# One slot for the widest weights, fewer copy transfers, and evenly spread preparation steps in a hybrid DeltaNet and attention layer

## The chip, the cores and the metric

The kernel runs on one core of a Trainium2 chip. A core has five engines that work side by side: TensorE (PE in the profile, its weight loads PEld), VectorE (DVE), ScalarE (ACT), GpSimd (POOL) and SyncE (SP), which issues most DMA transfers. The metric is the device time of one execution in microseconds (us); lower is better. The engines are tied to each other by semaphores: an instruction that lacks an input waits, and so does everything behind it in its engine's queue.

## What is computed

The reference is one layer of a transformer over 1024 latent tokens and 256 context tokens of width 1024:

```python
px = modulate(rms_norm(x, norm1_w[i]), sh1, sc1) @ w_in[i]
pc = modulate(rms_norm(ctx, norm1_w[i]), csh1, csc1) @ w_in[i]
dn_c, s_ctx_f, s_ctx_b = gated_deltanet(pc[..., :DN_IN], ...)
dn_x, _, _ = gated_deltanet(px[..., :DN_IN], ..., s_ctx_f, s_ctx_b)
na_x = neighborhood_attention(qx, kx, vx, kc, vc, na_rpb[i], rows)
x = x + g1 * (jnp.concatenate([dn_x, na_x], axis=-1) @ w_out[i])
x = x + g2 * swiglu(modulate(rms_norm(x, norm2_w[i]), sh2, sc2), w_ffn_in[i], w_ffn_out[i])
```

The columns of the input projection go to two groups. Group A (gated DeltaNet) has 4 heads: a short convolution and SiLU on q, k and v, then a scan over chunks of the sequence, forward and backward. Each chunk needs the inverse of a triangular matrix built from k, the decay and beta. Group B has 8 heads of attention over a window of the 64-wide latent grid together with all context keys.

## The kernel before, in words

**Jobs.** The projection is a list of jobs, worked off in a loop over `n` (L1050 and on). A `Block` makes 128 columns for all tokens: its product (`mm`, L405) runs in 8 parts `k`, each of 6 matmuls (queries, two token segments) or 9 (keys and values, three segments). A `Wide` makes 256 or 272 columns, token tile by token tile (`wide`, L595, 24 matmuls a tile; 10 tiles for the attention's values, 8 for the gate z). In order: `k0 k1 k2 k3 z1 | nk0 nk1 nk2 nv0 nk3 | q0..q3 | nq0..nq3 v0 nv1 | v1 v2 v3 z0`. The number of nk0's job is `inv`, of nq0's `later`, of nv1's `values`. After its product a job is evacuated by ACT (L438, L453), gets SiLU or squares, in the next round a `norm`, two rounds later a `finish`, which for values transposes (L527), scales on DVE (L531) and stores to HBM (L535, array `v_d`).

**Norm of attention keys and queries.** `norm` (L490 to L493) takes for each segment a PSUM bank named "m", does one matmul (L492) and takes the logarithm from the bank on ACT (L493). Keys have three segments. There are two "m" banks, two "pr" banks and four "blk" banks in that phase.

**Background steps.** Two generators run beside the jobs, by `bg.step` (L1090, L1096): `block_inverses` (43 steps: decay tables; masks; an elimination on DVE over 30 columns, L885 and L887, two columns a step; a memset, L891; transposes back on PE, L897; a store to `x_d`) and then `preps` (10 preparations of two chunks each, 8 steps each; matmuls L967, L968, L987, L998 in "pr" banks, stores to `at_d` and `y_d`, L1010). The first two preparations may run early; the other eight wait until all q jobs are finished, which is so from nq2 on. They need 64 steps. A block gives 8 steps, a wide tile 2, a tile of nv1 3. What remains is drained ahead of v3 (L1061).

**Order.** Where no order is written out by hand, the framework's planner orders each engine's instructions: those that come first in the code go first, unless its model says that their inputs are not ready, in which case later ones pass. So the queues differ from the order in the code, and a queue waits where the model was wrong.

**Weights.** Every weight block goes from HBM into the one slot `wraw` (L195, L586), is rounded into a high part by ACT (L199, L587) and its remainder taken by POOL (L200, L588). The Wide jobs' high and low parts lie in one slot `zw` in the pool `zp`, but z0's lie in a new pool `sp1`, opened when `zp` and all other pools of the phase have been closed (L1063 to L1066).

**The turn to the next phase.** With nv1 done, 64 transfers of 64 KB copy its rows from `nv_d` to the window layout `vw_d` (L1104 to L1109) on SP's queue. Ahead of v3 the attention generator `fill` starts its loads (L260, L262, L263: qs, kh, kl). With z0 the PSUM pools change (L1070): z0's product and the attention's first scores (L303) share the new banks. Then the scan starts.

Of the kernel before, what the change touches and what calls it, by code (L numbers as in the profile page):

```python
# [9 lines left out]
F32 = mybir.dt.float32  # L10
F32R = mybir.dt.float32r
# [9 lines left out]
KT = 8  # L21
# [67 lines left out]
def hybrid(ctx, tc, a, dbg):  # L89
# [45 lines left out]
        dve.memset(bias[:, i:i + 1], v)  # L135
    b_eps, b_naq = bias[:, 0:1], bias[:, 1:2]
    mr = const("mr", [128, 5, 128], F32R)
    mneg = const("mneg", [128, 2, 128], F32R)

    v_d = dram.tile([T, 512], F32, name="v_d", tag="v_d")  # L140
    k_d = dram.tile([T, 512], F32, name="k_d", tag="k_d")
# [233 lines left out]
    with ExitStack() as bs:  # L375
# [32 lines left out]
        class Block:  # L408
# [64 lines left out]
            def norm(self):  # L473

                kind, acc, t0, i = self.kind, self.acc, self.t0, self.i
                if kind == "v":
                    return
                if kind == "k":
                    sp.dma_start(kT_d[:, :, i], acc.rearrange("p (c t) -> p c t", t=128))
                    return  # L480
                r = self.r
                if kind == "q":
                    sp.dma_start(qT_d[:, :, i], acc[:, t0:].rearrange("p (c t) -> p c t", t=128))
                    p = bank()
                    for c in range(8):
                        pe.matmul(p[:, c:c + 1], r[:, t0 + c * 128:t0 + (c + 1) * 128], M[C_ONE][:, 0:1],
                                  start=True, stop=True)
                    dve.tensor_copy(SQ[:, :, i], p[:, 0:8])
                    return
                for s0, n in self.segs:  # L490
                    p = bank()
                    pe.matmul(p[:, :n], M[C_BD2], r[:, s0:s0 + n], start=True, stop=True)  # L492
                    act.activation(r[:, s0:s0 + n], p[:, :n], AF.Ln, bias=b_eps, scale=1.0 / ND)  # L493
                if kind == "nq":
                    act.activation(r[:, t0:], r[:, t0:], AF.Exp, scale=-0.5, bias=b_naq)
                else:
                    act.activation(r[:, t0:], r[:, t0:], AF.Exp, scale=-0.5)
                isk = kind == "nk"
                u = acc
                dve.scalar_tensor_tensor(u[:, t0:], u[:, t0:], qkw[:, isk:isk + 1], r[:, t0:],  # L500
                                         op0=OP.mult, op1=OP.mult)
                hl16 = cp.tile([128, 2, T], F16, name="hl16", tag="kx", bufs=3)
                h16, l16 = hl16[:, 0], hl16[:, 1]
                if isk:
                    act.copy(h16, u)
                    dve.tensor_tensor(l16, u, h16, OP.subtract)
                else:
                    for hf in range(2):
                        s = slice(t0 + hf * 512, t0 + hf * 512 + 512)
                        uv = u[:, s].rearrange("p (r b c) -> p b r c", r=8, b=4)  # L510
                        hv, lv = (x[:, s].rearrange("p (b r c) -> p b r c", b=4, r=8) for x in (h16, l16))
                        act.copy(hv, uv)
                        dve.tensor_tensor(lv, uv, hv, OP.subtract)
                for i, x in enumerate((h16, l16)):
                    for hb in range(2):
                        hd = 2 * self.i + hb
                        dst = nk_d[i, hd] if isk else nq_d[hd, i]
                        sp.dma_start(dst, x[hb * 64:hb * 64 + 64, t0:])

            def finish(self):  # L520
                kind, acc, i = self.kind, self.acc, self.i
                if kind in "kv":
                    vt = cp.tile([128, NCH, 128], F32, name="vt", tag="kx", bufs=3)
                    for g, m in ((0, 4), (4, 4), (8, 2)):
                        p = bank()
                        for c in range(m):
                            pe.transpose(p[:, c * 128:(c + 1) * 128], acc[:, (g + c) * 128:(g + c + 1) * 128], ident)  # L527
                        if kind == "k":
                            act.copy(vt[:, g:g + m].rearrange("p c d -> p (c d)"), p[:, :m * 128])
                        else:  # L530
                            dve.tensor_tensor(vt[:, g:g + m], p[:, :m * 128].rearrange("p (c d) -> p c d", d=128),  # L531
                                              SV[:, g:g + m, i:i + 1].to_broadcast([128, m, 128]), OP.mult)
                        yield
                    dst = v_d if kind == "v" else k_d
                    sp.dma_start(dst[:, i * 128:(i + 1) * 128].rearrange("(c p) d -> p c d", p=128), vt)  # L535
                if kind == "q":
                    kT = cp.tile([128, T], F32, name="kTh", tag="kx", bufs=3)
                    sp.dma_start(kT.rearrange("p (c t) -> p c t", t=128), kT_d[:, :, i])
# [25 lines left out]
        class Wide:  # L564


            def __init__(self, kind, half, zp):
                self.kind, self.half, self.zp = kind, half, zp
                self.n = 272 if kind == "z" and half else 256
                self.lasting = kind == "z" and not half  # L570

            def room(self):
                w = self.zp().tile([128, 2, KT, 256 if self.lasting else 272], F32R, name="zw", tag="zw")
                self.hi, self.lo = w[:, 0], w[:, 1]

            def prefetch(self):
                h2, n = 2 * self.half, self.n // 2
                src = a["w_nv"] if self.kind == "nv" else a["w_z%d" % self.half]
                if self.kind == "z":
                    h2 = 0  # L580
                if not self.lasting:
                    self.room()
                for i in range(2):
                    raw = wp.tile([128, KT, 136], F32, name="wraw", tag="wraw", bufs=1)
                    r, s = raw[:, :, :n], slice(i * n, i * n + n)
                    sp.dma_start(r, src[h2 + i])  # L586
                    act.copy(self.hi[:, :, s], r)  # L587
                    pool.tensor_tensor(self.lo[:, :, s], r, self.hi[:, :, s].bitcast(F32), OP.subtract)  # L588
# [55 lines left out]
        with ExitStack() as xs:  # L644
# [65 lines left out]
            with tc.manual_schedule(engines={mybir.EngineType.PE, mybir.EngineType.DVE, mybir.EngineType.Activation}):  # L710
# [30 lines left out]
                for k in range(1, KT):  # L741
# [11 lines left out]
                                ada(q, act.copy)  # L753
                    if k == 5:
                        act.copy(mr[:, 4], ident)
                        for d in range(2):
                            act.mul(mneg[:, d], masks[:, d], -1.0e30)
                        act.copy(mr[:, 0:4], masks)

        cp = pools(bs, "cp", "right")  # L760
        late = ExitStack()
        adp = pools(late, "adp", "left")
        zpool = [pools(late, "zp", "left")]
        first_half = ExitStack()
# [4 lines left out]
        def zp():  # L769
            return zpool[0]  # L770

        def decay_tables(gp):
            def small(name):
# [51 lines left out]
        def block_inverses():  # L825
            with ExitStack() as gs:
# [55 lines left out]
                for c in range(30, 0, -1):  # L882
                    w = 31 - c
                    t = tt[:P, :, :c * w].rearrange("p b (r j) -> p b r j", j=w)
                    dve.tensor_tensor(t, N[:P, :, 0:c, c:c + 1].to_broadcast([P, 4, c, w]),  # L885
                                      N[:P, :, c:c + 1, c + 1:32].to_broadcast([P, 4, c, w]), OP.mult)
                    dve.tensor_tensor(N[:P, :, 0:c, c + 1:32], N[:P, :, 0:c, c + 1:32], t, OP.add)  # L887
                    if c % 2:
                        yield
                flat = N.rearrange("p b r c -> p b (r c)")  # L890
                dve.memset(flat[:P, :, 0:1024:33], 1.0)  # L891
                yield
# [134 lines left out]
                        yield  # L1027
                flush(tick[0] + 2)

        jobs = first + [Block("k", 2), Block("k", 3), Wide("z", 1, zp)]  # L1030
        inv = len(jobs)
        jobs += [Block("nk", i) for i in range(3)] + [Wide("nv", 0, zp), Block("nk", 3)]
# [4 lines left out]
        jobs += [Block("nq", i) for i in range(4)] + [Block("v", 0), Wide("nv", 1, zp)]  # L1037
        values = len(jobs) - 1
        jobs += [Block("v", i) for i in (1, 2, 3)] + [Wide("z", 0, zp)]

        def blk(n):
            return jobs[n] if 0 <= n < len(jobs) and isinstance(jobs[n], Block) else None
# [9 lines left out]
        for n in range(2, len(jobs) + 2):  # L1052
# [7 lines left out]
            if n == len(jobs) - 2:  # L1060
                bg.drain()  # L1061
                bg2.drain()
                late.close()  # L1063
                sp1 = pools(middle, "sp1", "left")
                zpool[0] = sp1
                jobs[n + 1].room()  # L1066
                fill = attention(pools(attn, "nw", "left", 2))
                next(fill)
            if final:
# [7 lines left out]
            if isinstance(j, Wide):  # L1077
                for t, _ in enumerate(j.tiles()):
# [4 lines left out]
                    if t == 4 and nrm:  # L1083
# [3 lines left out]
                        fin = nrm.finish()  # L1087
                        done.add(n - 1)
                        nrm = None
                    bg.step(3 if n == values else 2)  # L1090
            elif j:
                for k in range(KT):
                    j.mm([k])
                    if k >= 3:
                        next(fin, 0)
                    bg.step(1)  # L1096
                    if n > inv + 4:
                        bg2.step(1)
                j.evac()
# [3 lines left out]
            if isinstance(j, Wide) and n == values:  # L1103
                vlat = nv_d[CT:].rearrange("(r c) d -> r c d", c=64)  # L1104
                for cb in range(4):
                    for ch in range(4):
                        for r in range(4):
                            sp.dma_start(vw_d[r * 32:r * 32 + 32, :, cb, ch],
                                         vlat[4 * ch + r, BLKS[cb]:BLKS[cb] + 32].rearrange("c (h d) -> c h d", d=128))  # L1109
            if nrm:  # L1110
                nrm.norm()
            if isinstance(j, Block):
# [665 lines left out]
```

## Time and profile before

| | us |
|---|---|
| median of 3 runs | 1546.32 (1540.7 to 1547.51) |
| the profiled execution | 1549.54 |
| its span, first to last instruction | 1547.5 |
| PE busy in the span | 1479.8 (96%) |
| DVE busy | 994.3 (64%) |
| ACT busy | 727.7 (47%) |

The profile's page begins with the busy time of each engine and a picture of the span in 40 slices, in which "PEclk" is the clock granted to TensorE in tenths of full speed. A busy PE at half clock makes half the progress. Further views are the waits (who waited for whom, in sum), the timeline (instructions in order of time; at the end of a row, in brackets, the idle time before it and what ended it; "SPq" and "ACTq" rows are DMA issues), and windows (busy time and granted clock of a stretch).

### The profile page before, as it was taken

To read this page: it belongs to the slowest core of one execution; us is meant where nothing else is said; L and a number is where in the kernel's file an instruction comes from. 1 tells how busy PE (TensorE), PEld (TensorE's weight loads), DVE (VectorE), ACT (ScalarE), POOL (GpSimd) and SP (SyncE) were. 2 spreads that over 40 slices of the span, in tenths; PEclk is the share of its full clock that TensorE was granted. 3 is DMA by queue.
4 is the path that set the end of the run, shared out by engine and by line. 5 is a ranking of instruction groups with operands and counts; after the bars stand their busy time and mean duration, and the time that the engine had idled before them with its cause. 6 is when DMAs were issued, how large, how long until landed. Compare 5 with 4: busy or idle time off the path is not lost. (4 is left out here: it accounts for less than half of the span.)

```text
span 1547.5 us, 23963 instructions
## 1 busy us (share of the span) xinstructions
PE 1479.8 (96%) x8702; PEld 1235.2 (80%) x8702; DVE 994.3 (64%) x1712; ACT 727.7 (47%) x1404; POOL 233.6 (15%) x286
## 2 busy tenths in 40 slices
PE   6999999899989978999999999999999999999998
PEld 3788787678778867888887878888888888888887
DVE  5774497675554543777986469866665556599652
ACT  5442552635764235666773166333333334354440
POOL 1154500733554010111210000000000000000000
PEclk9999999999999979999999999999999999999999
DMA  9274221577556467899637502632323324698742
GB/s 389 64 217 133 67 72 63 163 212 241 182 169 212 130 174 237 283 288 261 220 102 255 208 34 82 211 102 103 103 102 103 109 100 159 231 381 279 244 144 82
DMA packets 204118, 267.35 MB, mean 173 GB/s; under 512 B 16736, under 2 KB 114528, under 8 KB 202976
## 3 DMA queue, kind: packets, MB, share of 16 engines
q1 hardware_dynamic: 198480, 261.07, 51.7%
q10 hardware_dynamic: 5520, 4.76, 0.9%
q8 instruction: 68, 1.11, 0.3%
q14 instruction: 50, 0.41, 0.1%
HBM read 201.02 MB, written 68.94 MB: 174 GB/s over the span
## 5 line engine op out<-in xcount | busy, mean ns | idle before, releaser
L405 PE MATMUL blk<-hh,whi 128*128 128x512 f32 (+1 forms) x410 | 123.4, 395 | 2.3 <-ACT kk L550 1.4
L1415 ACT CAST uhi<-wq 128x512 fp32r<-128x512 f32 x101 | 61.0, 622 | 133.5 <-issue 84.6
L1415 ACT CAST uhi<-ws 128x512 fp32r<-128x512 f32 x91 | 53.9, 621 | 147.3 <-PE ps L1354 92.9
L405 PE MATMUL blk<-hl,whi 128*128 128x512 f32 (+1 forms) x410 | 116.8, 377 | 0.3 <-DVE hl L707 0.3
L595 PE MATMUL blk<-zw,hh 128*128 128x256 f32 (+1 forms) x576 | 115.0, 293 | 1.3 <-ACT kk L550 1.1
L405 PE MATMUL blk<-hh,wlo 128*128 128x512 f32 (+1 forms) x410 | 114.7, 377 | 0.6 <-POOL wlo L200 0.6
L1416 DVE TENSOR_TENSOR ulo<-wq,uhi 128x512 fp32r<-128x512 f32 x101 | 67.4, 687 | 59.1 <-ACT uhi L1415 34.0
L1354 PE MATMUL ps<-hT,uhi 128*128 128x512 f32 x336 | 103.7, 390 | 0.0
L1354 PE MATMUL ps<-hT,ulo 128*128 128x512 f32 x336 | 103.5, 389 | 0.0
L1354 PE MATMUL ps<-lT,uhi 128*128 128x512 f32 x336 | 103.4, 389 | 0.0
L595 PEld LDWEIGHTS blk<-zw,hh 128*128 128x128 f32 x576 | 92.8, 192 | 5.2 <-ACT kk L550 1.4
L1354 PE MATMUL ps<-hB,uhi 128*128 128x512 f32 x288 | 89.2, 391 | 0.6 <-ACT hB L1529 0.6
L1354 PE MATMUL ps<-lB,uhi 128*128 128x512 f32 x288 | 88.7, 389 | 0.4 <-DVE lB L1530 0.4
L1354 PE MATMUL ps<-hB,ulo 128*128 128x512 f32 x288 | 88.7, 389 | 0.0
L405 PEld LDWEIGHTS blk<-hh,wlo 128*128 128x128 f32 x410 | 72.6, 192 | 15.3 <-POOL wlo L200 0.9
L405 PEld LDWEIGHTS blk<-hl,whi 128*128 128x128 f32 x410 | 72.4, 191 | 14.5 <-DVE hl L707 0.8
L405 PEld LDWEIGHTS blk<-hh,whi 128*128 128x128 f32 x410 | 69.4, 194 | 18.2 <-issue 4.5
L595 PE MATMUL blk<-zw,hl 128*128 128x256 f32 (+1 forms) x288 | 83.2, 289 | 0.0
L1354 PEld LDWEIGHTS ps<-lT,uhi 128*128 128x128 f32 x336 | 63.1, 188 | 13.1
L1354 PEld LDWEIGHTS ps<-hT,ulo 128*128 128x128 f32 x336 | 63.1, 188 | 13.1
L1354 PEld LDWEIGHTS ps<-hT,uhi 128*128 128x128 f32 x336 | 62.9, 188 | 13.0
L200 POOL TENSOR_TENSOR wlo<-wraw,whi 128x1024 fp32r<-128x1024 f32 x18 | 44.7, 2485 | 179.2 <-ACT whi L199 160.7
(359 smaller groups left out, 3540.5 us busy)
## 6 DMA issues: line engine op xcount, KB each, us to landing
wq<-w_fo SPq DMA_DIRECT2D x99, 256.0 KB, 4.2
wq<-w_gu SPq DMA_DIRECT2D x88, 256.0 KB, 2.9
wad<-wa SPq DMA_DIRECT2D x64, 256.0 KB, 4.4
bt<-rpb SPq DMA_DIRECT2D x64, 192.0 KB, 3.8
t_d<-g SPq DMA_DIRECT2D x22, 512.0 KB, 3.6
fr<-t_d SPq DMA_DIRECT2D x44, 256.0 KB, 5.0
f_d<-g SPq DMA_DIRECT2D x33, 256.0 KB, 2.1
fr<-f_d SPq DMA_DIRECT2D x33, 256.0 KB, 3.8
```

The costliest lines, as they stand in the source:

```text
L200: lo_engine.tensor_tensor(o, r, h.bitcast(F32), OP.subtract)
L405: pe.matmul(o, ww[:, k], xx[k][:, s], start=k == 0 and j == 0, stop=k == KT - 1 and j == 2)
L595: pe.matmul(p[:, :c1 - c0], x[k][:, s], ww[:, k, c0:c1], start=k == 0 and j == 0, stop=k == KT - 1 and j == 2)
L1354: pe.matmul(o, w[wi][:, k], x[xi][:, k], start=first and k == 0 and j == 0, stop=k == n - 1 and j == 2, skip_group_check=True)
L1415: act.copy(hi, self.raw[key])
L1416: dve.tensor_tensor(lo, self.raw[key], hi.bitcast(F32), OP.subtract)
```

## The change

Seven edits. (1) The third segment of a key block's norm takes a "pr" bank. (2) `sp1` is opened at the start, below the pools that close, and holds one `zw` slot of 272 columns for all four Wide jobs. (3) `mneg`, a constant of the preparations, moves to a pool that closes with the phase and is computed a little later. (4) The stores to `v_d` are issued by ACT, not SP. (5) `block_inverses` yields twice more ahead of its memset. (6) nv1's tiles give 2 steps; blocks from nq0 on give 10, the added ones at `k` of 2 and 6. (7) The 64 copies to `vw_d` become 16 of 256 KB.

```diff
-                for s0, n in self.segs:
-                    p = bank()
+                for j, (s0, n) in enumerate(self.segs):
+                    p = bank("pr" if j == 2 else "m")
...
-                    sp.dma_start(dst[:, i * 128:(i + 1) * 128].rearrange("(c p) d -> p c d", p=128), vt)
+                    (act if kind == "v" else sp).dma_start(dst[:, i * 128:(i + 1) * 128].rearrange("(c p) d -> p c d", p=128), vt)
...
             def room(self):
-                w = self.zp().tile([128, 2, KT, 256 if self.lasting else 272], F32R, name="zw", tag="zw")
+                w = sp1.tile([128, 2, KT, 272], F32R, name="zw", tag="zw")
...
-                        for d in range(2):
-                            act.mul(mneg[:, d], masks[:, d], -1.0e30)
                         act.copy(mr[:, 0:4], masks)
...
+        sp1 = pools(middle, "sp1", "left")
         adp = pools(late, "adp", "left")
-        zpool = [pools(late, "zp", "left")]
+        mneg = adp.tile([128, 2, 128], F32R, name="mneg", tag="mneg")
+        for d in range(2):
+            act.mul(mneg[:, d], mr[:, d].bitcast(F32), -1.0e30)
...
                     if c % 2:
                         yield
+                yield
+                yield
                 flat = N.rearrange("p b r c -> p b (r c)")
                 dve.memset(flat[:P, :, 0:1024:33], 1.0)
...
                 late.close()
-                sp1 = pools(middle, "sp1", "left")
-                zpool[0] = sp1
-                jobs[n + 1].room()
                 fill = attention(pools(attn, "nw", "left", 2))
...
-                    bg.step(3 if n == values else 2)
+                    bg.step(2)
...
-                    bg.step(1)
+                    bg.step(1 + (n >= later and k in (2, 6)))
...
-                        for r in range(4):
-                            sp.dma_start(vw_d[r * 32:r * 32 + 32, :, cb, ch],
-                                         vlat[4 * ch + r, BLKS[cb]:BLKS[cb] + 32].rearrange("c (h d) -> c h d", d=128))
+                        sp.dma_start(vw_d[:, :, cb, ch].rearrange("(r c) h d -> r c h d", c=32),
+                                     vlat[4 * ch:4 * ch + 4, BLKS[cb]:BLKS[cb] + 32].rearrange(
+                                         "r c (h d) -> r c h d", d=128))
```

More of the change, by code (lines that the diff above doesn't have):

```diff
@@ L137, in hybrid @@
     mr = const("mr", [128, 5, 128], F32R)
-    mneg = const("mneg", [128, 2, 128], F32R)
     v_d = dram.tile([T, 512], F32, name="v_d", tag="v_d")
@@ L564, in hybrid, with __init__ @@
         class Wide:
-            def __init__(self, kind, half, zp):
-                self.kind, self.half, self.zp = kind, half, zp
+            def __init__(self, kind, half):
+                self.kind, self.half = kind, half
                 self.n = 272 if kind == "z" and half else 256
-                self.lasting = kind == "z" and not half
             def room(self):
-                w = self.zp().tile([128, 2, KT, 256 if self.lasting else 272], F32R, name="zw", tag="zw")
+                w = sp1.tile([128, 2, KT, 272], F32R, name="zw", tag="zw")
                 self.hi, self.lo = w[:, 0], w[:, 1]
@@ L580, in prefetch @@
                     h2 = 0
-                if not self.lasting:
-                    self.room()
+                self.room()
                 for i in range(2):
@@ L1028, in preps @@
                 flush(tick[0] + 2)
-        jobs = first + [Block("k", 2), Block("k", 3), Wide("z", 1, zp)]
+        jobs = first + [Block("k", 2), Block("k", 3), Wide("z", 1)]
         inv = len(jobs)
-        jobs += [Block("nk", i) for i in range(3)] + [Wide("nv", 0, zp), Block("nk", 3)]
+        jobs += [Block("nk", i) for i in range(3)] + [Wide("nv", 0), Block("nk", 3)]
         turn = len(jobs)
@@ L1036, in hybrid @@
         queries = range(turn, later)
-        jobs += [Block("nq", i) for i in range(4)] + [Block("v", 0), Wide("nv", 1, zp)]
+        jobs += [Block("nq", i) for i in range(4)] + [Block("v", 0), Wide("nv", 1)]
         values = len(jobs) - 1
-        jobs += [Block("v", i) for i in (1, 2, 3)] + [Wide("z", 0, zp)]
+        jobs += [Block("v", i) for i in (1, 2, 3)] + [Wide("z", 0)]
         def blk(n):
```

2 lines of the change are left out of this document (removed).

## The prediction

> **What bounds the kernel now.** I read the page's busy times and PEclk first, then PE's waits in the projection (150 to 600 us, the only part that the edits reach), the SP queue there, and windows with the granted clock.
>
> ```profile
> span 1547.5 us, 23963 instructions
> PE 1479.8 (96%) x8702; PEld 1235.2 (80%) x8702; DVE 994.3 (64%) x1712; ACT 727.7 (47%) x1404; POOL 233.6 (15%) x286
> PEclk9999999999999979999999999999999999999999
> ...
> PE m L492 <- ACT cr L493: 5.3, 4, 1.4
> PE pr L967 <- POOL rg L957: 2.9, 3, 1.2
> PE m L897 <- DVE N L891: 2.9, 1, 2.9
> PE sc L303 <- DMA kh<-nk_d: 4.5, 1, 4.5
> PE sc L303 <- DVE mx L305: 4.1, 1, 4.1
> PE sc L314 <- DVE bt L309: 2.3, 1, 2.3
> ...
> 548.50:595.30 46.80, 35.66 (x264) 32.38 (x264) 20.30 (x31) 16.84 (x29) 5.27 (x4) 0.82 0.60 167
> 552.30:569.40 17.10, 9.81 (x44) 7.64 (x45) 12.05 (x18) 6.74 (x10) 3.16 (x3) 0.50 0.87 245
> 258.80:265.60 6.80, 6.80 (x38) 6.10 (x37) 0.69 (x1) 3.41 (x8) 0.00 (x0) 0.50 0.01 2
> 430.00:496.00 66.00, 60.42 (x540) 53.55 (x539) 35.66 (x45) 35.80 (x75) 33.04 (x45) 1.00 0.62 192
> 195.00:258.00 63.00, 57.48 (x373) 50.60 (x371) 60.06 (x64) 24.19 (x35) 5.46 (x2) 1.00 0.20 59
> ```
>
> PE is busy 96% of the span, so the change can win only idle PE time and half-clock time. In the window rows the columns are length, then busy time of PE, PEld, DVE, ACT and POOL, then the clock. The weakest stretch is 548.5 to 595.3, where z0 and the attention's start share PE: 46.80 us with 35.66 busy, at a mean clock of 0.82. Three waits (4.5, 4.1, 2.3 us; sum 10.9) are nearly all of the 11.1 idle, and the clock stood at 0.50 for 17.10 us from 552.3.
>
> **Where that stall comes from.** The timelines of SP, ACT, POOL and PE:
>
> ```profile
> 495.88 36.09 SPq L1108 DMA_DIRECT2D vw_d<-nv_d  x53
> 533.18 2.42 SPq L1010 DMA_DIRECT2D y_d<-y  x4
> 535.68 0.61 SPq L586 DMA_DIRECT2D wraw<-w_z  x1
> 545.47 0.37 SPq L535 DMA_DIRECT2D v_d<-vt  x1
> 545.93 0.63 SPq L260 DMA_DIRECT2D qs<-nq_d  x1
> 555.34 0.60 SPq L586 DMA_DIRECT2D wraw<-w_z  x1
> ...
> SPq L535 <- DVE vt L531: 9.1, 1, 9.1
> ...
> 517.64 2.38 POOL L200 TENSOR_TENSOR wlo<-wraw,whi 128x1024 fp32r<-128x1024 f32 x1 [17.36 <-PE pr L998]
> 548.13 1.35 ACT L453 COPY cr<-blk 128x256 f32<-128x256 f32 x3 [5.77 <-PE blk L405]
> 549.35 1.07 ACT L587 CAST zw<-wraw 128x1024 fp32r<-128x1024 f32 x1
> 550.50 2.34 POOL L588 TENSOR_TENSOR zw<-wraw,zw 128x1024 fp32r<-128x1024 f32 x1 [11.30 <-ACT zw L587]
> 563.15 2.37 POOL L588 TENSOR_TENSOR zw<-wraw,zw 128x1024 fp32r<-128x1024 f32 x1 [10.31 <-ACT zw L587]
> ...
> 553.04 0.58 PE L303 MATMUL sc<-kh,qs 128*128 128x256 f16 x2 [4.54 <-DMA kh<-nk_d]
> 563.38 0.56 PE L595 MATMUL blk<-zw,hh 128*128 128x256 f32 x1
> ```
>
> 53 of the 64 copies keep SP until 532. Behind them stand the last stores, then the first half of z0's weights (535.68), then a store of v1 that waits 9.1 us for DVE, then the attention's loads (545.93). So when v3's product ends at 548.5 PE has neither keys nor z0's weights; z0's second half is loaded at 555.34 and finished by POOL after 563.
>
> **The change part by part.** The sum is made against the profiled execution, 1549.54 us; that is 3.22 above the median of the runs shown.
>
> *Copies, `v_d` on ACT, the `zw` slot (one term).* 64 issues become 16. A copy now costs SP 36.09/53 = 0.68 us. Four times the bytes might cost more; the store of 640 KB in row L535 keeps SP 0.37 us, so I take 16 x 0.68 = 11 us at most, ending near 507 (lower end 16 x 0.37; upper end, if the cost goes with the bytes, 64 x 0.68 as today). The last preparation's stores then go out when ready, about 521. `wraw` is free when POOL ends at 517.64+2.38 = 520.0. Two halves one after the other, each with a load, an ACT cast (1.07) and a POOL pass (2.37):
>
> ```profile
> wraw<-w_z SPq DMA_DIRECT2D x2, 512.0 KB, 5.3
> 141.63 0.62 PE L405 MATMUL blk<-hh,whi 128*128 128x256 f32 x2 [1.39 <-ACT kk L550]
> ```
>
> 2 x (5.3+1.07+2.37) = 17.5, so z0's weights stand at about 537.5, 11 us ahead of need. The single slot adds no wait: its last reader, nv1, is done by 496. The attention's loads no longer queue behind the 9.1 us. z0 comes earlier in the code than the scores, so PE should go on with its tiles and the scores' waits for DVE fall beside them. Next in line is the change of PSUM pools: v3's banks must be evacuated. The nearest row is the other change of pools, 1.39 us of idle PE at 141.63. The gain: 10.9 of waits, plus half of the 9.81 busy us that ran at half clock (4.9), minus 1.4: **14.4**. Ends: 15.8 (no wait at the change) and 0 (z0 late for another reason).
>
> The ACT issue itself takes about as long as SP's 0.37 us, four times, on an engine busy 47%: nothing on the path. What stands behind it is a rival below. `mneg`: two small ACT copies, a few us later than now and over 200 us before their first use: nothing; the covers are gone only if ACT were the bound.
>
> *The third bank.* In four key norms PE waits 5.3 us in all, because the third matmul needs the bank that ACT still reads. With a "pr" bank it goes at once. But PE then only arrives earlier at what it waits for next. The first and the last of the four, and between them the first such place, the transposes behind the inverse:
>
> ```profile
> 181.32 1.12 PE L492 MATMUL m<-cr,cst 128*128 128x512 f32 x2 [1.37 <-ACT cr L493]
> 273.35 1.12 PE L492 MATMUL m<-cr,cst 128*128 128x512 f32 x2 [1.27 <-ACT cr L493]
> ...
> 257.70 0.45 PE L897 MATMUL m<-cst,N 80*128 80x80 f32 x2 [2.89 <-DVE N L891]
> ...
> 221.10:235.60 14.50, 14.50 (x119) 14.14 (x119) 1.00 0.30 83
> ```
>
> DVE is busy 60.06 of 63 us from 195 to 258: the inverse is a DVE chain. The first norm wait is ahead of the chain's start and carries on (1.4). The two in the middle (5.3-1.4-1.3 = 2.6) are likely to be added to the 2.89, the fourth (1.3) to the L967 waits of 2.9. I take **1.4**; ends 5.3 (all carries) and -1.7 (nothing does, and the longer wait draws another 3.4 us at half clock).
>
> *Two empty steps.* The transposes already run one block behind their place in the code, held by DVE; a later place moves nothing. **0**. Ends: 6.3 (the 2.89 and half of the 6.80 at 0.50 go) and below nothing (two steps of half a wide tile each, if the steps did pace it). The window row above is nv0 alone, L595 with 119 matmuls in 14.50 us, 0.122 each: a tile of 24 takes 2.9, so that end is -2.9.
>
> *Even steps.* The eight preparations need 64 steps. Now nq2, nq3, v0, nv1, v1, v2 give 8+8+8+30+8+2, then 10+10+10+20+10+4: both end in v2, so nothing is left to drain. PE's waits of that stretch:
>
> ```profile
> PE pr L998 <- ACT kk L990: 1.2, 2, 0.6
> PE pr L987 <- DVE kk L974: 1.1, 2, 0.8
> PE blk L405 <- ACT cacc L438: 0.9, 1, 0.9
> ...
> L987 PE MATMUL pr<-fx,kk 128*128 128x128 f32 x63 | 8.3, 280 | 5.5 <-ACT y L1001 2.5 <-ACT kk L990 2.3 <-DVE y L1000 0.7
> ```
>
> nv1's 30 steps carry 5.5 us. In proportion 20 carry 3.7 (gain 1.8); with all of it gone, 5.5. The 24 steps of nq2, nq3 and v0 carry 3.2; 30 would carry 4.0 (loss 0.8). So 1.0 to 4.7; the two longest waits come from ACT, and thinning helps most there: **2.5**. Lower end -5.5, as much again.
>
> Sum: 14.4 + 1.4 + 0 + 2.5 = 18.3. 1549.5 - 18.3 = 1531.2 for a profile, and 1546.3 - 18.3 = **1528.0** as a median. Past 600 us I expect the same stages, shifted.
>
> **A rule against a row.** A 2.89 us wait was followed by 6.80 us at clock 0.50, while nv1's waits (2.5 and 2.3 us, window 430 to 496) left the clock at 1.00. The Trainium skill, "TensorE: Matmul & The Clock Gate", section "Why this matters for your kernels", puts the limit at idle gaps of about 3 us. By that rule a wait of 2.9 us costs only itself; the trace differs at L897, and the 6.3 us used below stands on the row.
>
> **Rivals.**
> - *Everything carries.* All norm waits, the inverse's wait with its half clock, and the pacing: 5.3+6.3+4.7+15.8 = 32.1, 1514.2 us. For: the two steps stand right ahead of the place that waits. Against: DVE's 60.06 of 63.
> - *The copies still hold SP* (the edit does not do what it says): a transfer of four times the bytes takes four times as long on SP. Gain 1.4+2.5 = 3.9, 1542.4 us. Against: 640 KB in 0.37 us.
> - *ACT is held by the `v_d` issues.* On SP three of them wait 22.0 us:
>
> ```profile
> SPq L535 <- DVE vt L531: 22.0, 3, 12.6
> ```
>
>  If ACT stood as long, z0's evacuation behind it would stop PE, less one tile of 2.9 us that the second bank covers each time: 22.0-8.7 = 13.3 lost, sum 5.0, 1541.3 us. Against: ACT is idle 5.77 us at 548 anyhow, and the planner places the issue where it expects the data. The Trainium skill, "PSUM — Partial Sum Buffer", section "Engine vs sequencer instructions", calls ScalarE's queue strictly first in, first out. By that rule nothing behind a waiting issue could pass, and this rival's time would follow.
> - *The doubled steps stall PE* (slower). With preparations live there are nine places where two steps come together (two each in nq2, nq3, v0, v1, one in v2); if one costs what L897 does, 2.89 and half of 6.80, that is 6.3. From five of them on, 31.5-18.3 = +13.2, 1559.5 us; it decides at the fifth (four give +6.9, within 0.5%). For: L897. Against: nv1 took 30 such steps for 5.5 us with the clock at 1.00.
>
> **Chances and range.** Forecast 0.58, everything carries 0.17, SP held 0.11, ACT held 0.05, doubled steps 0.09. A measurement of this kernel tells 0.5% (7.7 us) from nothing. Faster: 0.58+0.17 = 0.75; same: 0.11+0.05 = 0.16; slower 0.09. The range goes from 1513 (everything carries) to 1544 (SP held, and 1.6 for the pacing); the forecast's own is 1519 to 1536.
>
> **What would show it.** In the profile after: `vw_d` x16 within some 11 us of SP; z0's second load before 535; L595 of z0 starts some 1.4 us after v3's last L405, ahead of any L303; no window at 0.50 there; no L303 wait for kh. L492 no longer waits, while L897 waits 5 us rather than 2.9. L987 waits under 4 us in nv1. The prediction is wrong if z0's weights or the new banks come later than I reckon, if ACT shows idle time ended by "DVE vt", or if the early part draws new half-clock stretches.

## The result and the profile after

The changed kernel takes 1589.01 us in the median of 4 runs (1586.71 to 1596.7), the kernel before, run beside it, 1546.91 (1540.7 to 1550.22). The ratio over all runs is 1.0286, with a 95% interval from 1.0237 to 1.0334: 2.9% slower, where 1.2% faster had been forecast. The profiled execution of the changed kernel took 1587.66 us, its span is 1585.9, 38.4 more than before.

Rows from the page of the changed kernel, then PE's longest waits from 500 to 600 us (who waited for whom, us in total, times, longest), and windows with the columns of before. Line numbers behind 137 have moved by one to seven: L1101 is the copies' line, L995 was L998, L302 was L303, L592 was L595.

```profile
span 1585.9 us, 23909 instructions
PE 1484.0 (94%) x8702; PEld 1238.8 (78%) x8702; DVE 991.1 (62%) x1712; ACT 732.1 (46%) x1407; POOL 237.8 (15%) x286
PEclk9999998899899959999999999999999999999999
...
PE pr L995 <- POOL y L974: 23.1, 1, 23.1
PE sc L302 <- DMA kh<-nk_d: 6.9, 1, 6.9
PE sc L302 <- DVE mx L304: 5.7, 1, 5.7
...
548.50:595.30 46.80, 10.30 (x75) 6.81 (x74) 10.31 (x16) 7.06 (x12) 5.63 (x13) 0.55 0.64 192
553.20:601.00 47.80, 12.64 (x84) 9.45 (x85) 12.18 (x20) 9.09 (x14) 8.62 (x15) 0.50 0.62 185
```

PE's work is nearly the same, 1484.0 us busy for 1479.8. The stretch in which the prediction wanted to win 14.4 us is where the time went: from 548.5 to 595.3 PE is busy for 10.30 us, where it was 35.66 before, and from 553.2 on the clock stands at half for 47.80 us, where it was 17.10. The waits of 23.1, 6.9 and 5.7 us take the place of 4.5, 4.1 and 2.3.

What held PE is read backwards through four engines. PE's L995, a late preparation, waits for POOL (L974); POOL for a store of `y_d`; that store stands on SP behind the copies. Rows from the timelines of SP, ACT, POOL and PE, then SP's longest wait, the copies as a group (shortest, median and longest time on SP in ns, first and last start), and the DMA view of 506 to 525 us:

```profile
502.12 63.56 SPq L1101 DMA_DIRECT2D vw_d<-nv_d  x15
565.77 3.29 SPq L1007 DMA_DIRECT2D y_d<-y  x2
571.44 0.62 SPq L583 DMA_DIRECT2D wraw<-w_z  x1
580.26 0.51 SPq L261 DMA_DIRECT2D kh<-nk_d  x1
...
547.68 0.38 ACTq L534 DMA_DIRECT2D v_d<-vt  x1
...
572.49 2.65 POOL L974 COPY y<-xc 32x128 f32<-32x128 f32 x8 [49.81 <-DMA y_d<-y]
...
573.81 4.51 PE L995 MATMUL pr<-y,kk 128*32 128x32 f32 x48 [23.09 <-POOL y L974]
...
SPq L1101 <- DMA v_d<-vt: 25.0, 1, 25.0
...
L1101 SPq DMA_DIRECT2D vw_d<-nv_d x15: 592/2951/3177, 502.1 to 562.7; - x15
...
q1 hardware_dynamic: 3242, 1.65, 28.7%
```

15 of the 16 copies hold SP for 63.56 us, where 53 of the 64 had held it for 36.09. Two things make that up. A copy of 256 KB keeps SP for 2.95 us in the median: 256 KB in 2.95 us is 89 GB/s, and the DMA view moves 88 GB/s at 28.7% of 16 engines' time (4.6 engines). And in the middle SP waits 25.0 us for the store of v1 to `v_d`, which ACT issues at 547.68. The last preparation's stores come at 565.77, z0's weights at 571.44, the attention's keys at 580.26; the prediction had the stores out at about 521, z0's weights ready at 537.5, and no wait for the keys.

The copy has nothing to do with `v_d`: it reads `nv_d` and writes `vw_d`. The changed program's own list of waits shows why it waits. In it each transfer that SP or ACT issues gets one of eight completion semaphores in turn, and an issue waits until the last user of its semaphore is done:

```
409 L534 DMA v_d<-vt 128x10x128 [waits DMAHW3_49,DVE_49]
...
222 L1101 DMA vw_d<-nv_d 512x1x128 [waits DMAHW1_49]
223 L1101 DMA vw_d<-nv_d 512x1x128 [waits DMAHW2_49]
224 L1101 DMA vw_d<-nv_d 512x1x128 [waits DMAHW4_49]
...
230 L1101 DMA vw_d<-nv_d 512x1x128 [waits DMAHW2_49]
231 L1101 DMA vw_d<-nv_d 512x1x128 [waits DMAHW3_49]
```

The first row is from ACT's queue, the others are from SP's. Number 3 of the first round has gone to v1's store, so the copies go from 2 to 4. One round later a copy is due for number 3, and it waits for that store.

### The profile page after: what moved, and what is told of

It is laid out like the page before. It is cut to its first block, busy times and chain, and to the rows that moved or that the text cites. A ratio compares the mean times of both kernels' runs of the same rounds, so it can differ in the third digit from the quotient of the medians.

```text
span 1585.9 us, 23909 instructions
## 1 busy us (share of the span) xinstructions
PE 1484.0 (94%) x8702; PEld 1238.8 (78%) x8702; DVE 991.1 (62%) x1712; ACT 732.1 (46%) x1407; POOL 237.8 (15%) x286
## 5 line engine op out<-in xcount | busy, mean ns | idle before, releaser
L592 PE MATMUL blk<-zw,hh 128*128 128x256 f32 (+1 forms) x576 | 114.1, 293 | 0.0
L592 PEld LDWEIGHTS blk<-zw,hh 128*128 128x128 f32 x576 | 93.1, 193 | 3.2 <-issue 1.2
L404 PEld LDWEIGHTS blk<-hl,whi 128*128 128x128 f32 x410 | 72.9, 193 | 14.4 <-DVE hl L704 0.8
L592 PE MATMUL blk<-zw,hl 128*128 128x256 f32 (+1 forms) x288 | 82.6, 287 | 0.0
L199 POOL TENSOR_TENSOR wlo<-wraw,whi 128x1024 fp32r<-128x1024 f32 x18 | 47.9, 2664 | 199.9 <-ACT whi L198 175.9
L304 DVE CUSTOM_DVE_ANT_0 bt<-sc,bt 128x640 f32<-128x640 f32 x64 | 52.6, 821 | 37.0 <-DMA bt<-rpb 17.0
```

The costliest lines, as they stand in the source:

```text
L199: lo_engine.tensor_tensor(o, r, h.bitcast(F32), OP.subtract)
L304: dve.tensor_tensor_reduce(bt, sc[:, u * 640:u * 640 + 640], bt, -1.0, 3.0e38, OP.add, OP.min, m[:, 0:1])
L404: pe.matmul(o, ww[:, k], xx[k][:, s], start=k == 0 and j == 0, stop=k == KT - 1 and j == 2)
L592: pe.matmul(p[:, :c1 - c0], x[k][:, s], ww[:, k, c0:c1], start=k == 0 and j == 0, stop=k == KT - 1 and j == 2)
```

## The experiments

Two theories stood after the result. **E**: the copies' new cut moves them over few DMA engines, so that SP stands for as long as the data does. **W**: moving `v_d` to ACT's queue makes SP wait for transfers that ACT issues late. A third, **P**, blamed the even pace.

### One cause taken out of the changed kernel at a time

Run a_copies64 gives the changed kernel its 64 copies back. Run a_copies_r keeps 16 copies of 256 KB, but cuts them by row group instead of by channel:

```diff
-                    for ch in range(4):
-                        sp.dma_start(vw_d[:, :, cb, ch].rearrange("(r c) h d -> r c h d", c=32),
-                                     vlat[4 * ch:4 * ch + 4, BLKS[cb]:BLKS[cb] + 32].rearrange(
-                                         "r c (h d) -> r c h d", d=128))
+                    for r in range(4):
+                        sp.dma_start(vw_d[r * 32:r * 32 + 32, :, cb],
+                                     nv_d[CT:].rearrange("(q r c) d -> r q c d", r=4, c=64)[
+                                         r, :, BLKS[cb]:BLKS[cb] + 32].rearrange("q c (h d) -> c h q d", d=128))
```

Run a_vd_sp moves `v_d` back to SP, and a_oldpace restores the old steps (3 for a tile of nv1, 1 at every `k`).

> The changed kernel with the 64 copies of 64 KB back. Theory E (engines): a 256 KB copy of the changed kernel runs on few of the 16 DMA engines, because its source is cut into 4 rows, and holds SP 2.95 us. 64 copies at 0.64 hold SP 41 us instead of the 47 that 16 copies take, so little comes back from the issues alone: 1575 to 1585. Theory W (wait): SP stands 25 us in the middle of the copies for the store of v_d that ACT issues later; with the 64 copies this wait stays or moves, and the time stays at 1580 to 1590. Theory P (pace): the stores of the seventh preparation's y fall behind the copies since nv1's steps are thinner; the stall of 23 us in front of L995 stays while the copies are long: 1575 to 1590.

> The changed kernel with 16 copies of the same 256 KB cut the other way: each takes one grid row in four with 32 columns, so that the outermost cut is 128 pieces on both sides and not 4. Theory E: each copy then uses all 16 engines and holds SP for about 0.7 us, all of them under 20 us; the stores behind them go out by 525, the 23 us stall in front of L995 and most of the 47 us at half clock go: 1530 to 1550. Theory W: SP still waits for the store of v_d until about 550: 1575 to 1590. Theory P: the stall goes if the copies are short, as under E.

> The changed kernel with the stores to v_d back on SP. Theory W: the 25 us wait inside the copies goes, SP ends the copies near 549 instead of 565, and the stall before z0 shrinks by 15 us or so, with the half clock: 1560 to 1570. Theory E alone: the copies still take 47 us, and the store that now waits on SP for DVE holds it as long: 1580 to 1590.

> The changed kernel with the old pace: 3 steps per tile in nv1 and 8 per block. Theory P: the seventh preparation's stores go out ahead of the copies, the last preparation ends near 525 and PE no longer waits 23 us at L995; but z0's weights still come behind the copies, so only part comes back: 1565 to 1580. Theories E and W: z0's weights and the attention's keys still come after 570, so PE waits the same time for them instead: 1580 to 1590.

| run | median us | ratio to the kernel before, 95% |
|---|---|---|
| the changed kernel | 1589.01 | 1.0286 (1.0237 to 1.0334) |
| a_copies64 | 1558.33 | 1.0047 (1.0031 to 1.0063) |
| a_copies_r | 1563.49 | 1.0093 (1.0057 to 1.0129) |
| a_vd_sp | 1570.16 | 1.0129 (1.0099 to 1.0159) |
| a_oldpace | 1581.72 | 1.0203 (1.0180 to 1.0227) |

The copies in a_copies_r as a group, SP's longest wait there and the DMA view of 503 to 513 us (packets, MB, share of 16 engines); behind them two rows of a_vd_sp:

```profile
L1101 SPq DMA_DIRECT2D vw_d<-nv_d x16: 571/656/2051, 496.1 to 513.7; - x16
...
SPq L583 <- DMA v_d<-vt: 30.9, 1, 30.9
...
q1 hardware_dynamic: 5060, 2.53, 96.3%
```

```profile
L1101 SPq DMA_DIRECT2D vw_d<-nv_d x15: 653/2951/3437, 508.7 to 549.0; - x15
...
PE sc L302 <- DMA kh<-nk_d: 9.7, 1, 9.7
```

The same 256 KB in another cut costs SP 0.66 us in the median, not 2.95: so it is the cut, not the bytes (E). Nor is it the size of the packets: they have about 500 bytes in both (1.65 MB in 3242, 2.53 MB in 5060), but they keep 96.3% of the 16 engines' time busy instead of 28.7%. With SP free early the wait for v1's store only moves, from a copy to the load of z0's weights, where it lasts 30.9 us (W). With `v_d` back on SP that wait is gone, but the copies still keep SP until 552. Either repair alone brings back more than half of the 2.9%. a_vd_sp came out at the upper end of where W had it (1560 to 1570), a_oldpace where both E and W had it (1580 to 1590). a_copies_r missed both of its ranges (above E's, below W's): the slow copies were gone and W's wait was not. a_copies64 came out far below every expectation: in its trace SP does not wait for `v_d` at all from 440 to 620 us, though ACT still issues v1's store, at 553.36. Taking out the slow copies took out W's wait as well, which none of the theories had reckoned with.

The Trainium skill, "DMA: Bandwidth & Descriptors", section "Why a DMA increments its semaphore by 16 and not by 1", says that a transfer is spread over the largest number of engines up to 16 that divides the slowest dimension of both sides. In the program the cut by channel has 4 as the slowest size of its source and 512 of its destination; the cut by row group has 128 (32 columns of 4 head pairs each, one stride). By that rule the first runs on 4 engines and the second on 16; the traces agree nearly, with 4.6 and 15.4 of 16 engines busy by the shares above, and 2.95 us against 0.66.

### Parts of the change alone, in the kernel before

Each run makes one edit of the change in the kernel before and nothing else; a_copies_r_vd_sp is the changed kernel with both causes out.

> The kernel before (64 copies vw_d<-nv_d, v_d stored by SP) with the change's 16 copies and nothing else. Theory E (16 copies of 256 KB whose slowest dimension is 4 rows move on few DMA engines, 2.95 us of SP each): 16 x 2.95 = 47 us of SP where there were 64 x 0.68 = 44, and every load behind them is slow as well while the train lasts; z0's first weights after 540 us, the attention's start later by some 5 to 15 us: 1555 to 1567 us. Theory W (only the wait for v1's store by ACT on a shared completion semaphore costs): v_d is stored by SP here, so no wait of over 12 us for v_d<-vt, and 1548 to 1554 us, as before. The prediction's term (a copy costs 0.68 us whatever it carries): 1535 to 1541 us.

> The kernel before with 16 copies cut by row group and block, all 16 channels in one copy, so that the slowest dimension is 128 rows wide, and nothing else. E: a copy holds SP some 0.6 to 0.7 us, the train is 10 to 12 us long and ends near 507, z0's weights are there before 540, and the stretch from 548 to 595 us loses most of its 10.9 us of waits and its half clock: 1536 to 1542 us, the gain that the prediction booked. Theory C (the cover: with loads early PE still waits at z0 and the first scores for DVE and for the change of PSUM pools): waits of 5 us or more between 545 and 565 remain and draw half clock: 1546 to 1553 us.

> The kernel before with v_d stored by ACT and nothing else. W: a copy or a load on SP waits for a v_d<-vt that ACT issues late, 10 to 30 us, if the planned order lets it take the same completion semaphore; z0's second half or the attention's loads come later by some 5 us: 1551 to 1560 us. If ACT's issue is harmless and the 9.1 us wait of SP for DVE vt is simply gone: 1545 to 1551 us.

> The changed kernel with both suspects taken out: 16 copies whose slowest dimension is 128 rows wide, and v_d stored by SP. E and W together (these two are the whole loss and the rest is harmless): no wait on SP for v_d<-vt over 12 us, copies within 12 us of SP, no half clock over 10 us near 555: 1530 to 1542 us. E and W with theory P (the steps spread evenly cost 5 us in v1 by the waits near 426 to 432 and 462): 1541 to 1550. C (the cover): waits at z0 and the first scores stay, 1550 to 1558 us.

> The kernel before with the steps spread evenly and nothing else. The prediction's step: nv1's waits under L987 thin out, 1.0 to 4.7 us won, 1545 to 1549 us. Theory P (the even pace is what is left of the loss once copies and v_d are put right): the last preparation's y_d stores fall behind v1's product, they stand on SP ahead of z0's second load and of the attention's loads, and the doubled steps add 2 to 5 us of PE waits between 400 and 465 us: 1553 to 1562 us.

> The kernel before with the third bank and nothing else. The prediction's step: L492's 5.3 us go, 2.6 of them turn up in the wait at L897, net 1.4 won: 1547 to 1550 us. Rival: the longer wait at L897 draws a longer half-clock stretch (10.2 us for 6.8), net 0 to 3 lost: 1550 to 1553 us.

> The kernel before with the two empty steps in the inverse and nothing else. The prediction's step: 0, L897 still waits 2.9 us for N (DVE's chain sets it): 1549 to 1552 us. Rival: the wait at L897 and its half clock go: 1543 to 1546 us. Rival on the other side: later steps push the later preparations back: 1552 to 1556 us.

> The kernel before with the one lasting slot for the widest weights (and mneg in its new place) and nothing else: 64 copies, v_d on SP, old pace, old bank. The prediction: no wait is added, 1549 to 1552 us. Theory S (the slot itself costs: z0's weights find their place late, or the order of the engines around it is worse): 1554 to 1562 us. With P the two should add up to the 12.6 us that remained with copies and v_d put right.

| run | edit alone | median us | ratio, 95% |
|---|---|---|---|
| b_copies16 | 16 copies, the change's cut | 1558.49 | 1.0059 (1.0039 to 1.0080) |
| b_copies_r | 16 copies, by row group | 1551.62 | 1.0023 (1.0003 to 1.0043) |
| b_vd_act | `v_d` on ACT | 1553.44 | 1.0010 (0.9989 to 1.0031) |
| b_pace | even steps | 1556.58 | 1.0041 (1.0021 to 1.0062) |
| b_bank | third bank | 1550.19 | 1.0004 (0.9991 to 1.0016) |
| b_empty | two empty steps | 1548.79 | 0.9993 (0.9982 to 1.0005) |
| b_slot | one slot, `mneg` | 1549.40 | 0.9998 (0.9983 to 1.0013) |
| a_copies_r_vd_sp | all but the two causes | 1562.69 | 1.0077 (1.0048 to 1.0107) |

Bank, empty steps and slot are nothing, to 0.2%. The copies, `v_d` and the pace alone add up to 1.1%, so 1.8% of the loss belongs to none alone. And a_copies_r_vd_sp, expected at 1558 at most by every theory, stays 0.8% slow. The pace (0.41%) and the good cut (0.23%) add up to 0.64%, which lies within its interval; in its profile PE waits 9.9 us at z0's first matmul for ACT's cast, to which the text comes back below. b_copies16 came out where E had it, b_pace where P had it, and b_copies_r in the range of theory C. b_vd_act lies in W's range, but its interval does not tell it from no change.

*The pace.* Window 380 to 480 us and PE's waits in it, first b_pace and then the kernel before:

```profile
380.00:480.00 100.00, 86.12 (x588) 68.13 (x587) 52.06 (x55) 61.69 (x117) 50.98 (x56) 0.91 0.55 167
...
PE pr L967 <- ACT y L1001: 5.1, 2, 2.7
PE pr L967 <- DVE y L1000: 2.6, 1, 2.6
PE pr L998 <- ACT kk L990: 2.3, 2, 1.7
PE pr L998 <- DVE y L1000: 2.3, 1, 2.3
PE pr L987 <- DVE kk L974: 1.5, 2, 1.3
```

```profile
380.00:480.00 100.00, 91.28 (x698) 74.60 (x697) 57.80 (x62) 65.83 (x125) 54.41 (x60) 1.00 0.59 180
```

nv1's two long waits at L987 (2.5 and 2.3 us) are gone, as the prediction had it. In their place stand waits at L967 and L998 in nq2 to nv1. All PE waits of the window come to 13.8 us where the rows of before give 8.7, and the clock, which stood at 1.00, is 0.91. One execution each would not show the clock's part, since it differs from run to run with the same steps; but in the seven profiles with even steps this window has 0.91 to 0.95, in the thirteen with the old steps 0.95 to 1.00. In this execution, 1563.5 us and so at the upper end of its runs, PE finishes v3 11.6 us later than before. That is the prediction's rival of the doubled steps.

*Why the good cut alone won nothing.* With SP free at 511 and z0's first load at 526.80, PE in b_copies_r still idles at v3's end. SP, ACT and the windows of that run:

```profile
495.38 15.81 SPq L1107 DMA_DIRECT2D vw_d<-nv_d  x16
526.80 0.61 SPq L586 DMA_DIRECT2D wraw<-w_z  x1
545.67 0.37 SPq L535 DMA_DIRECT2D v_d<-vt  x1
561.35 0.60 SPq L586 DMA_DIRECT2D wraw<-w_z  x1
...
548.33 1.35 ACT L453 COPY cr<-blk 128x256 f32<-128x256 f32 x3 [5.74 <-PE blk L405]
556.70 1.27 ACT L468 ACTIVATE cacc<-cacc 128x1280 f32<-128x1280 f32 x1 [7.02 <-DVE cacc L461]
557.87 1.03 ACT L587 CAST zw<-wraw 128x1024 fp32r<-128x1024 f32 x1
...
548.50:595.30 46.80, 33.00 (x240) 29.10 (x240) 18.17 (x31) 17.07 (x28) 5.27 (x4) 0.78 0.58 162
```

The first half of the weights is issued at 526.80 and ACT rounds it at 557.87. In ACT's queue the cast stands behind v3's evacuation (548.33) and its SiLU, which waits 7.02 us for DVE; in the kernel before it stood ahead of that SiLU, at 549.35. The shorter train freed SP at 511 where it had been 532, and z0's first load went out 9 us earlier than the 535.68 of before, but its cast came 8.5 us later. The second half goes through the same slot `wraw` and is loaded only at 561.35 (555.34 before). The attention's loads still stand behind v1's store (545.67). PE gained nothing. Theory C had the size right, but blamed DVE's convolution and the PSUM pools; ACT's place for the cast is a nearer cause, and the last runs test it.

### The two causes together

> The kernel before with the 16 copies of the change and v_d stored by ACT, nothing else. Theory I (the two need each other: a copy takes over the completion semaphore of v1's store, which ACT issues at about 548, so that the slow train is cut in two by a wait of 20 us or more and everything behind it comes past 565): 1570 to 1583 us, far above the sum of the two alone (+9 and +2). Theory A (the parts add up; what is missing comes from the pace and the slot): 1558 to 1563 us.

> The kernel before with the 16 copies, v_d stored by ACT and the steps spread evenly; no third bank, no empty steps, no single slot. If these three are the whole of it: 1583 to 1596 us, as the changed kernel. If the slot, the bank or the empty steps are needed as well: 1565 to 1580 us.

b_copies16_vd took 1578.90 us, ratio 1.0189 (1.0148 to 1.0229), where theory I had it; b_three, with the pace, 1586.33, ratio 1.0246 (1.0210 to 1.0281), where it should lie if the three were the whole. The longest waits of SP and of PE in b_copies16_vd:

```profile
SPq L1107 <- DMA v_d<-vt: 25.6, 1, 25.6
...
PE sc L303 <- DMA kh<-nk_d: 31.6, 1, 31.6
```

The two parts that cost 0.6% and 0.1% alone cost 1.9% together, and with the pace 2.5%, which the interval does not tell from the changed kernel's 2.9%. Alone, v1's store on ACT is waited for by a load of the attention's keys, behind the copies and z0's first weights (9.8 us in b_vd_act), and alone the copies' train runs through to 539. Together the wait falls into the middle of the train, and all the rest of it comes behind.

### Moving the cast

If ACT's place for the cast is what holds z0, a priority for z0's weights should win what the prediction booked on the copies:

```diff
-                jobs[n + 1].prefetch()
+                with tc.high_priority() if n == len(jobs) - 2 else ExitStack():
+                    jobs[n + 1].prefetch()
```

The priority holds for all of `prefetch`: the two loads on SP, the casts on ACT and the passes on POOL.

> A version of the kernel before with the single slot, 16 copies whose slowest dimension is 128 rows wide, and z0's weights given a high priority in the planner, so that ACT rounds them ahead of v3's copies (old pace, old bank, v_d on SP). Theory C as the reason why shorter copies alone won nothing (ACT rounds z0's weights only behind v3's last copy, whenever they land, and the second load waits for that): with the cast ahead PE goes on with z0 when v3's product ends, the 4.5 us wait for kh and most of the half clock near 552 are gone: 1533 to 1543 us. If something else holds the stretch (DVE's convolution of v3, the change of PSUM pools): 1546 to 1552 us.

> The single slot and z0's early cast, but with the 64 copies of before. If the copies' count matters once z0's weights no longer stand behind them: z0's second load comes a few us before 545, its first tiles wait, and the time is that of before, 1548 to 1551 us. If only the place of the cast matters: as with 16 good copies, 1543 to 1548 us.

> 16 good copies and z0's early cast, but z0's weights in the old place, over the memory of the pools that close. If the slot is what lets the early cast work: ACT waits for the last preparation's tiles, the cast comes after 533 and holds v3's and v2's copies behind it, 1550 to 1565 us. If the slot has no part in it: 1543 to 1548 us.

> The kernel before with nothing but z0's early cast: 64 copies, v_d on SP, old pace, z0's weights in the old place. If the place of the cast alone carries the gain: 1533 to 1538 us, as with the single slot (0.9905 of before there). If the single slot is needed: ACT's cast waits for the last preparation's memory, 1543 us or more.

| run | copies | slot | median us | ratio, 95% |
|---|---|---|---|---|
| c_z0_early | 16 by row group | one | 1545.76 | 0.9976 (0.9956 to 0.9997) |
| c_z0_noslot | 16 by row group | old | 1546.05 | 0.9966 (0.9950 to 0.9982) |
| c_z0_64 | 64 | one | 1534.90 | 0.9905 (0.9884 to 0.9926) |
| b_z0_early | 64 | old | 1535.44 | 0.9895 (0.9875 to 0.9914) |

The last is the kernel before with the two lines above and nothing else, and it beats both kernels. Its window, the loads on SP, the casts on ACT, and z0's first matmul:

```profile
548.50:595.30 46.80, 40.20 (x334) 36.50 (x332) 23.20 (x44) 23.25 (x40) 2.62 (x9) 0.97 0.90 257
...
521.48 0.61 SPq L586 DMA_DIRECT2D wraw<-w_z  x1
530.54 0.60 SPq L586 DMA_DIRECT2D wraw<-w_z  x1
...
526.61 1.05 ACT L587 CAST zw<-wraw 128x1024 fp32r<-128x1024 f32 x1 [3.71 <-DMA wraw<-w_z]
534.70 1.04 ACT L587 CAST zw<-wraw 128x1024 fp32r<-128x1024 f32 x1 [1.80 <-DMA wraw<-w_z]
551.11 1.35 ACT L453 COPY cr<-blk 128x256 f32<-128x256 f32 x3 [3.92 <-PE blk L405]
...
552.51 0.39 PE L595 MATMUL blk<-zw,hh 128*128 128x256 f32 x1 [1.03 <-ACT cr L453]
```

Both loads now go out in the middle of the copies' train (521.48 and 530.54, where they went at 535.68 and 555.34), both halves are rounded by 536, PE starts z0 1.03 us behind v3, and the clock stays at 0.97 in a stretch where it was 0.82. So what wins is the load and the cast together; that the first load alone is not enough, b_copies_r shows, and a run that moves the casts alone was not made. The slot is not needed for it, and the fewer copies are in the way: with 64 copies the gain is 14 us, with 16 of the good cut 4. c_z0_64 so ran well below both of its expectations, c_z0_early fell between its two; c_z0_noslot and b_z0_early came out where the slot has no part. One of SP's waits in c_z0_early may be a reason; the stage at z0 itself runs well there too:

```profile
548.50:595.30 46.80, 38.47 (x323) 34.35 (x321) 21.25 (x44) 21.37 (x38) 1.63 (x5) 1.00 0.72 201
...
SPq L271 <- DMA z_d<-zg: 13.1, 1, 13.1
```

A load of the attention's biases again waits for a store that ACT issues late, z0's own to `z_d`, whose completion semaphore it takes over in this program. c_z0_noslot has the same wait (11.9 us), the two runs with 64 copies have none over 1.2: another count of transfers has dealt the semaphores in another way. By the last matmul of L592 z0 ends 13.2 us earlier than before, the scan's first matmul comes 11.1 earlier, and at the scan's end 3.3 are left. How the scan gives back the other 8 was not settled.

## Why the prediction was wrong, point by point

- **Copies: 16 x 0.68 = 11 us at most.** This is the step that failed first; with the next one it makes 1.9% of the 2.9%. I priced a copy by a store of 640 KB that keeps SP 0.37 us. That row shows a single transfer outside a train, in another cut. In the train SP is held as long as the data moves: 2.95 us a copy, 89 GB/s. The upper end I named, 64 x 0.68 = 44 us "if the cost goes with the bytes", was right in size (15 copies, 42 us, in b_copies16), but it was then given only to the rival "the copies still hold SP", and priced at no loss: b_copies16 loses 0.6%.
- **`v_d` on ACT: nothing on the path.** The mechanism that I weighed, ACT standing at the issue, cost nothing: ACT issues v1's store in 0.38 us, and though in b_vd_act it stands 3.5 us for DVE's `vt` at that place, it still waits for PE behind it. What I did not look for is who waits for that store, though the row that I quoted as a gain, a 9.1 us wait on SP, was the same late data. With the store on another queue SP no longer waits for it at its own place, but wherever its semaphore comes round: 25.0 us, in the train.
- **z0's weights at 537.5.** Wrong, and for a reason of its own: the sum of load, cast and pass took no account of the place of the cast in ACT's queue. b_copies_r has the load at 526.80 and the cast at 557.87, so even copies of about the price that I expected win nothing here. The gain itself was there, on another edit: 14.4 predicted, 14.0 measured in b_z0_early, in whose profile z0 ends 12.0 us earlier. That the figures lie so close is in part luck.
- **The `zw` slot and `mneg`: nothing.** Right: 0.9998.
- **Third bank: 1.4, with the waits moved to L897.** Right in the mechanism, not in the 1.4. The L492 waits are gone, and the wait at the inverse's transposes grows:

```profile
PE m L897 <- DVE N L891: 5.7, 1, 5.7
PE m L875 <- DVE WK L868: 1.5, 1, 1.5
```

 In b_bank it is 5.7 for 2.9, and a new one of 1.5 us at L875 takes up the first of the four, which I let carry; the wait at L856 grows from 1.8 to 2.6. The net is 1.0004, within 0.2% of nothing.
- **Two empty steps: 0.** Right: 0.9993, and L897's wait stays at 2.9 us.
- **Even steps: 2.5 won.** Wrong in sign. The step that failed is the scaling "30 steps would carry 4.0 where 24 carry 3.2". In nq2 to nv1 PE now waits for ACT's and DVE's `y` at L967 and L998, and within the 100 us of these two executions four stretches at half clock come with it (17.0 us in all, none before). The rival "the doubled steps stall PE" was the right one; its price of 6.3 us at each of up to nine places was too high: the measured one is 0.4% for all of them.
- **The end point.** Forecast 1528, range 1513 to 1544, measured 1589. No rival held a loss at the copies: "the copies still hold SP", which came true in part, was booked as the same time. The forecast treated the copies, `v_d` and z0 as one term with a lower end of 0, so that a loss there was left out by construction.

## What to carry to other kernels

Price a merged transfer by its access pattern and in the train that it will stand in, not by a lone store; look at what the slowest dimension becomes. When an issue moves to another queue, list who re-uses its completion semaphore, since an in-order queue can stop for a transfer that it has no data from. And before a load is made earlier, find the instruction that consumes it in its engine's queue: two lines that moved z0's loads and casts ahead won what the merged copies, the new queue and the slot were booked for.

## What the runs showed of the hardware

- The same 256 KB from HBM to HBM cost the issuing engine 2.95 or 0.66 us in a train (medians of the changed kernel and of a_copies_r), by the cut alone.
- The clock can fall after waits that are shorter than those of the prediction. In b_pace two waits of 1.25 and 0.29 us, 1.2 us apart, were followed by 3.40 us at half clock, while in the kernel before one of 2.29 us was followed by none. Nor does one wait always cost the same: nv1 has the old steps in b_z0_early too, and there a wait of 2.76 us came with 10.20 us at half clock. The timeline and the window of each:

```profile
383.49 1.16 PE L987 MATMUL pr<-fx,kk 128*128 128x128 f32 x8 [1.25 <-DVE kk L974]
384.94 1.88 PE L987 MATMUL pr<-fx,kk 128*128 128x128 f32 x8 [0.29 <-DVE kk L974]
385.20:388.60 3.40, 3.40 (x19) 2.69 (x19) 2.38 (x5) 2.33 (x8) 0.00 (x0) 0.50 0.47 105
```

```profile
451.64 0.49 PE L987 MATMUL pr<-fx,kk 128*128 128x128 f32 x2 [2.29 <-ACT kk L990]
449.50:456.00 6.50, 4.30 (x42) 3.87 (x42) 5.32 (x7) 5.83 (x14) 3.92 (x4) 1.00 0.78 239
```

```profile
446.72 2.08 PE L987 MATMUL pr<-fx,kk 128*128 128x128 f32 x8 [2.76 <-ACT y L1001]
446.10:456.30 10.20, 8.90 (x43) 8.20 (x43) 7.71 (x9) 6.99 (x15) 2.66 (x5) 0.50 0.75 232
```

 In all the profiles every stretch of one clock between the first and the last is 3.4 us long or a whole multiple of it (10.20 is three). Where a wait falls among these steps may decide; no run was made for it, so that stays open.
